# A hybrid state-space and attention layer on one core: taps made from tiles on the chip, bias loaded in halves, spreads by transpose, token tiles loaded in pairs

## The chip, the core and the metric

The kernel runs on one core of a Trainium2 chip. A core has five engines with queues of their own: TensorE (PE, matrix products; its weight loads are shown as PEld), VectorE (DVE), ScalarE (ACT), GpSimd (POOL) and SyncE (SP, which here only issues transfers). Each engine works through its own queue in order and waits on semaphores for the others. The metric is the device time of one execution in microseconds; lower is better. The profile shows one execution; its times count from the first instruction.

## The reference

One layer on 2048 tokens of 1024 features, in float32. `rmsnorm(x)` goes through one input projection, whose columns feed two groups:

```
h    = rmsnorm(x, g_mix);  proj = h @ w_in              # 2048 x 2048: u | q | k | v, 512 each
# group A: diagonal complex state space, 32 groups of 16 channels, 64 states each
lam_bar = exp(lam*dt);  b_bar = ((lam_bar-1)/lam) * B
states  = scan(lam_bar, u @ b_bar);  y = Re(states . C) + d*u
y    = gelu(y);  y = y * sigmoid(y @ w_glu + b_glu)
# group B: each frame attends to its 64-frame chunk and the 8 before it
s    = q.k/8 + rel_bias[head, clip(distance, -128, 128)]   # masked outside the band
att  = softmax(s) @ v                                       # 8 heads of 64
x    = x + concat(rmsnorm(y, g_ssm), rmsnorm(att, g_att)) @ w_out
h2   = rmsnorm(x, g_ffn)
x    = x + (silu(h2 @ w_gate) * (h2 @ w_up)) @ w_down        # inner width 2816
out  = rmsnorm(x, g_final)
```

## The kernel before

Tokens lie on the free axis in blocks of 512 (`SB`), features on the 128 partitions. A float32 operand is split into a high part (ACT, a cast) and a low part (VectorE, the difference), and a product is three matmuls (`mm3`, hi.hi, hi.lo, lo.hi). Small products and transposes are done on plain float32. Line 78 is the helper through which all products go, line 81 the one for transposes. PE's instructions keep the order in which the code emits them; the other queues are ordered by a planner, which may put anything forward whose inputs and buffers are free by its own estimate, except for the few instructions that are pinned.

Three stages matter here.

The **start** (`u_phase`) projects the state-space columns, blocks 1, 2, 3, 0. A block has four groups of 24 matmuls (`group`, banks `ps` or `pf`). Its token tiles `xt` (L440, `in_xp`) and its rows `x` for the sums of squares (L449) come from DRAM. When a block's root mean squares are known (`newton`), `spread` brings them from one column per 128 tokens onto all partitions: four products of the column, broadcast, with the identity, into a bank `pp`. Between the groups, `long(n)` advances `ssm_prologue`, which computes the state-space constants on VectorE: powers of the eigenvalues, the output side `v` (L337 to L345), the input side `wt` (L347 to L351), and, after the start, the powers `a8` on POOL (L353 to L364), the taps `kt` (the first eight values of the impulse response, products of `v` and `bb`, both reloaded from DRAM across partitions, L370 to L392) and the transposes of `wt` (L288 to L297), which are written to DRAM as `bst`. Also in the start, the negated bias (`nb`, 768 values per head) is spread out in DRAM to `nbm`, a 128 x 640 tile per head (L521), and two corners of each tile are set to 1e30 (L524).

The **attention** (`att_phase`) takes 128 steps (block, head pair, head of the pair, quarter block), in each of which PE does the scores `sc`, the transposes `pt` of an earlier step's probabilities and, at the end of a head, the product with the values (`pj`). `load_nb` (L798) loads the next head's bias tile two steps ahead. After a head pair, `pv_scale` (L875) spreads the reciprocals of the softmax sums with four products against the identity. Between these, units advance on a timetable: `hT_unit` loads, scales and splits the next block's token tiles (L695 to L707; two buffers `xt`, the first three tiles and the other five in two units), `qk_unit` and `v_unit` project, and eight `ssm_unit`s load (`U`, `Bst`, `Tm`, `Vm`, L549), multiply, scan on POOL (L587 to L599), move the result (`XG`, L621) and multiply again. The raw weights go through two buffers `raw` while block 0 is processed; later blocks reload the split weights `wss`. The pools of the attention take the memory that the prologue's pool gives back, and a tile there waits for the last use of what lay in its place; the values' tiles `v0` come first in it.

The **rest** (`mix_phase`, feed-forward and down projection) is touched only where it spreads root mean squares: `norm`, `rstd_steps`.

## Time and profile before

| | |
|---|---|
| time, median of 3 runs | 2327.94 us (2321.54 to 2329.34) |
| profiled execution | 2328.99 us, span 2327.2 us, mean granted clock 0.973 |
| PE busy | 2197.0 us of the span |
| VectorE, ACT, POOL busy | 1545.0, 1004.7, 349.0 us |
| start, to the last spread of the projection | 0 to 116.6 us |
| first scores to last scores of the attention | 142.7 to 756 us |
| moved by DMA | 434.90 MB |

A timeline row of the profile gives the start in us, the time in us, engine, line, operation, output and inputs by the program's names, shapes and a count; in brackets stands how long the engine had idled before and what it waited for. A row of waits gives who waited for what, the total in us, how often, and the longest. A row of DMA issues gives the queue, the count, the size of one and the median time from issue to landing. A row of a tile gives the shortest, median and longest duration in ns, and the first and last start. A row of windows gives the stretch, its length, each engine's busy time, the granted clock of PE as a share of full speed, the DMA engines' busy share and GB/s.

### The profile page before, as it was taken

The page shows a single profiled execution, that of the slowest core. Times are in us where ns is not written, and L with a number is a line of the kernel's source. Part 1 is how long each engine was busy: PE and PEld are TensorE (multiplying, and loading weights), DVE is VectorE, ACT ScalarE, POOL GpSimd, SP SyncE. Part 2 cuts the span into 40 slices and gives each one's busy share as a digit, 9 for nine tenths or more (in the row PEclk, how much of TensorE's full clock was granted, in tenths as well). Part 3 has the DMA queues.
Part 4 walks back from the last instruction along what each step waited for, and adds up shares of the span by engine and source line. Part 5 has one row for each costly group of instructions (what it writes and reads, how often), then busy time and mean ns, then how long its engine had stood idle before and what let it go on. Part 6 is the DMA issues. An engine that isn't in the chain of part 4 may idle for free.

```text
span 2327.2 us, 30433 instructions
## 1 busy us (share of the span) xinstructions
PE 2197.0 (94%) x10712; PEld 1852.3 (80%) x10712; DVE 1545.0 (66%) x2695; ACT 1004.7 (43%) x1655; POOL 349.0 (15%) x814
## 2 busy tenths in 40 slices
PE   8878899999997899999999999999999989999997
PEld 6766688898986688878888887888888878888886
DVE  7746545756545756777776668666756477789766
ACT  4435445555556752253333336333333343353321
POOL 3237545466542000000000000000000000000000
PEclk9989899999998999999999999999999999999998
DMA  8967676775654434763554647555423297465641
GB/s 274 291 221 249 194 209 196 200 221 176 193 153 146 141 105 149 245 198 127 182 180 149 235 160 284 183 198 163 167 90 114 68 338 255 163 216 186 227 158 73
DMA packets 225329, 434.90 MB, mean 187 GB/s; under 512 B 43480, under 2 KB 70152, under 8 KB 218072
## 3 DMA queue, kind: packets, MB, share of 16 engines
q1 hardware_dynamic: 220312, 418.79, 55.0%
q0 software_dynamic: 4864, 14.17, 1.9%
q8 instruction: 84, 1.38, 0.2%
q14 instruction: 69, 0.57, 0.1%
HBM read 292.88 MB, written 132.15 MB: 183 GB/s over the span
## 4 chain that ended last, share of the span: by engine, by line
PE 82%; DMA 6%; DVE 6%; POOL 2%; ACT 2%; issue 1%; SPq 1%; DVEq 0%; ACTq 0%; POOLq 0%
PE X L78 20%; PE ps L78 19%; PE Y L78 10%; PE pf L78 10%; PE big L78 9%; PE W L78 5%; PE pj L78 5%; PE sc L78 2%; PE pt L81 2%; DMA xt<-in_xp 2%; DMA xt<-in_xt 1%; DVE lo L154 1%; SPq L549 1%; DMA nb<-nbms 1%; DMA hd<-wc 0%
## 5 line engine op out<-in xcount | busy, mean ns | idle before, releaser
L78 PE MATMUL X<-hi,c 128*128 128x512 f32 x1408 | 451.3, 391 | 8.5 <-DVE c L154 6.9
L78 PE MATMUL ps<-hd,hd 128*128 128x512 f32 (+1 forms) x1968 | 432.0, 382 | 6.1 <-ACT hd L154 3.7
L78 PEld LDWEIGHTS ps<-hd,hd 128*128 128x128 f32 x1968 | 359.3, 190 | 77.5 <-ACT hd L154 4.6
L78 PEld LDWEIGHTS X<-hi,c 128*128 128x128 f32 x1408 | 265.6, 189 | 65.2 <-DVE c L154 7.8
L78 PE MATMUL X<-lo,c 128*128 128x512 f32 x704 | 274.9, 390 | 0.0
L154 ACT CAST hd<-hd 128x1536 fp32r<-128x1536 f32 (+1 forms) x106 | 147.6, 1393 | 238.1 <-DMA hd<-hq 181.9
L78 PE MATMUL Y<-hi,c 128*128 128x512 f32 x704 | 224.1, 389 | 1.5 <-DVE u L1367 1.5
L154 DVE TENSOR_TENSOR hd<-hd 128x1536 fp32r<-128x1536 f32 (+1 forms) x106 | 174.1, 1645 | 28.8 <-ACT hd L154 28.1
L154 DVE TENSOR_TENSOR c<-S,c 128x512 fp32r<-128x512 f32 x176 | 120.9, 688 | 104.1 <-ACT c L154 104.1
L829 DVE CUSTOM_DVE_ANT_0 s<-sc,nb 128x640 f32<-128x640 f32 (+4 forms) x128 | 94.5, 738 | 110.9 <-PE sc L78 98.7
L1491 DVE TENSOR_TENSOR acc<-acc,ps 128x512 f32<-128x512 f32 x196 | 131.3, 684 | 53.0 <-PE ps L78 48.3
L1363 ACT COPY u<-X 128x512 f32<-128x512 f32 x132 | 77.6, 588 | 204.9 <-PE X L78 204.8
L78 PE MATMUL big<-m,woh 128*128 128x512 f32 x512 | 162.7, 400 | 0.0
L78 PE MATMUL pf<-hi,w 128*128 128x512 f32 x416 | 153.1, 420 | 8.9 <-ACT w L154 4.6
L154 ACT CAST c<-S 128x512 fp32r<-128x512 f32 x176 | 109.5, 622 | 118.3 <-PE Y L78 67.0
L78 PEld LDWEIGHTS Y<-hi,c 128*128 128x128 f32 x704 | 132.1, 188 | 29.3 <-DVE u L1367 1.9
L78 PEld LDWEIGHTS X<-lo,c 128*128 128x128 f32 x704 | 132.8, 189 | 27.7
L154 ACT CAST c<-raw 128x512 fp32r<-128x512 f32 x132 | 82.2, 623 | 149.4 <-PE Y L78 71.2
L78 PE MATMUL Y<-lo,c 128*128 128x512 f32 x352 | 137.0, 389 | 0.0
L832 ACT ACTIVATE s<-s,mn 128x640 f32<-128x640 f32 (+4 forms) x128 | 98.0, 765 | 77.2 <-DVE mn L829 76.5
L848 DVE TENSOR_TENSOR ptl<-pt,pth 128x640 fp32r<-128x640 f32 (+3 forms) x152 | 98.3, 647 | 45.8 <-ACT pth L847 44.1
L847 ACT CAST pth<-pt 128x640 fp32r<-128x640 f32 (+3 forms) x152 | 83.7, 551 | 94.8 <-PE pt L81 89.5
(441 smaller groups left out, 4229.3 us busy)
## 6 DMA issues: line engine op xcount, KB each, us to landing
w<-wss SPq DMA_DIRECT2D x36, 1024.0 KB, 6.7
hq<-g SPq DMA_DIRECT2D x140, 256.0 KB, 2.2
hd<-hq SPq DMA_DIRECT2D x42, 768.0 KB, 4.4
hd<-wc SPq DMA_DIRECT2D x42, 768.0 KB, 6.0
raw<-in_w_gate SPq DMA_DIRECT2D x44, 512.0 KB, 3.7
raw<-in_w_up SPq DMA_DIRECT2D x44, 512.0 KB, 4.1
wc<-px SPq DMA_DIRECT2D x66, 256.0 KB, 3.2
wss<-w SPq DMA_DIRECT2D x12, 1024.0 KB, 6.0
```

What stands on the lines that cost most here:

```text
L78: return self.tc.keep_in_program_order(self.tc.nc.tensor.matmul(*a, **b))
L81: return self.tc.keep_in_program_order(self.tc.nc.tensor.transpose(*a, **b))
L154: return nc.scalar.copy(hi, raw), nc.vector.tensor_tensor(lo, raw, f32(hi), op=ALU.subtract)
L549: ins = nc.sync.dma_start(out, in_)
L829: nc.vector.tensor_tensor_reduce(s[:, :nk].rearrange("p (a b) -> p a b", a=nch), ps[:, :nch, :half], hd.nb[:, nk - 1 :: -1].rearrange("p ( ...
L832: nc.scalar.activation(s[:, :nk], s[:, :nk], AF.Exp, bias=mn[:], scale=-1.0, accum_out=sums[sb, pr][:, hh, qp : qp + 1])
L847: nc.scalar.copy(pth[:, a:b, qp, :], pt[:, a:b, :])
L848: nc.vector.tensor_tensor(ptl[:, a:b, qp, :], pt[:, a:b, :], f32(pth[:, a:b, qp, :]), op=ALU.subtract)
L1363: nc.scalar.copy(u[:], ps[:])
L1491: V.tensor_tensor(a, a, ps[:], op=ALU.add)
```

## The change

1. **Spreads.** `spread`, `rstd_steps` and `pv_scale` use a transpose of the broadcast column in place of the product with the identity.
2. **Taps.** They are made from the tiles in which VectorE computes `bbr`, `bbi` and `v`: for each group the real and the imaginary part are two products over 64 partitions that add up in one bank. The reloads of `bb` and `v` and the DRAM tensor `bb` go. The taps are now emitted between the projection groups, one block of eight groups behind the block of `v` that they read, and the transposes move up between the first q and k products. The transposed blocks 0 and 1 take the buffers of `v`, blocks 2 and 3 those of `bc` and `small`.
3. **Bias.** The DRAM tensor `nbm` goes. Two tiles on the chip hold a head's bias in turn; their corners are set once on POOL, and a head's values come straight from `nb` in two loads, one for each half of the partitions, whose rows overlap in DRAM. Head 0 is loaded in the start.
4. **Token tiles.** Of tiles 3 to 7 of a next block, 3 is loaded alone, 4 and 5 and then 6 and 7 as pairs into the buffers `raw`.

```diff
-LONG = 1, 3, 2
+VO, WI, TA = range(3)
+LONGS = ((VO, 0),), ((VO, 1),), ((TA, 0), (VO, 2)), ((TA, 1), (VO, 3)), ((TA, 2), (WI, 0)), ((TA, 3), (WI, 1)), ((WI, 2),), ((WI, 3),)
...
 def spread(k, te, pb, o, c):
     for i in range(4):
-        te.matmul(pb[:, i * P : (i + 1) * P], o[:, c + i : c + i + 1].to_broadcast([P, P]), k.ident[:], start=True, stop=True)
+        te.transpose(pb[:, i * P : (i + 1) * P], o[:, c + i : c + i + 1].to_broadcast([P, P]), k.ident[:])
...
-            bst = k.t(p, "v" if b_ > 1 else "vg", [P, 9 if b_ > 1 else 8, 2, NS], bufs=2)[:, :8]
+            bst = (k.t(p, "v", [P, 9, 2, NS], bufs=2) if b_ < 2 else k.t(p, ("bc", "small")[b_ - 2], [P, 8, 2, NS]))[:, :8]
...
+        def taps(b_):
+            kt = k.t(p, "kt", [CH, 8, P], bufs=2)
+            gs = slice(8 * b_, 8 * b_ + 8)
+            pss = [k.t(k.pro_psum, "pp", [P, 512])[:].rearrange("p (a b) -> p a b", a=4) for _ in range(2)]
+            for q in range(4):
+                for c, bt in enumerate((bbr, bbi)):
+                    for g2, ps in enumerate(pss):
+                        rows = slice(g2 * NS, (g2 + 1) * NS)
+                        k.te.matmul(ps[:CH, q, :], bt[rows, 4 * b_ + q, :], vts[b_][c][rows, q, :L, :].rearrange("p k c -> p (k c)"), start=c == 0, stop=c == 1)
+            for g2, ps in enumerate(pss):
+                nc.scalar.copy(kt[:, g2::2, :], ps[:CH])
+            V.tensor_tensor(kt[:, :, :CH], kt[:, :, :CH], dm[:, gs], op=ALU.add)
+            nc.gpsimd.dma_start(S["kt"][:, gs, 1], kt[:])
...
             if n == 1:
-                corner = k.t(p1, "corner", [64, 64])
-                nc.gpsimd.memset(corner[:], 1e30)
-                nc.sync.dma_start(S["nbm"][:], bass.AP(S["nb"].tensor, S["nb"].offset + 1, [[768, H], [1, P], [1, 640]]))
+                bias_corners(k, S["nba"])
+                bias_rows(k, S, 0, S["nba"])
...
-            long(LONG[n - 1])
+            long(1)
...
-            now += [group(b, f, f in pf) for f in (1, 2)]
+            for f in (1, 2):
+                now.append(group(b, f, f in pf))
+                if n > 1:
+                    long(1)
...
+def bias_rows(k, S, h, nb):
+    src = bass.AP(S["nb"].tensor, S["nb"].offset + h * 768 + 65, [[1, 64], [1, 576]])
+    k.nc.sync.dma_start(nb[:64, 64:], src)
+    k.nc.sync.dma_start(nb[64:, :576], src)
+    return nb
...
+            def load(q, n=1):
+                t = k.t(aw, "raw", [P, 1024], bufs=2) if n > 1 else k.t(aw, "xt", [P, SB], bufs=XB)
+                nc.sync.dma_start(t[:].rearrange("p (q t) -> p q t", q=n), io["xt"][q * P : (q + n) * P, ts].rearrange("(q p) t -> p q t", p=P))
+                for m in range(n):
+                    xts[q + m] = t[:, m * SB : (m + 1) * SB]
+            if q0 == 0:
+                load(0)
+                load(1)
+            else:
+                load(q0)
+                for q in range(q0 + 1, q1, 2):
+                    load(q, 2)
...
-                k.ta.matmul(pb[:, i * P : (i + 1) * P], rb[:, i].rearrange("p h d -> p (h d)"), ident[:], start=True, stop=True)
+                k.ta.transpose(pb[:, i * P : (i + 1) * P], rb[:, i].rearrange("p h d -> p (h d)"), ident[:])
```

More of the change, by code (lines that the diff above doesn't have):

```diff
@@ L140, in rstd_steps @@
     for i in range(nt):
-        te.matmul(pb[:, i * P : (i + 1) * P], o[:, i : i + 1].to_broadcast([P, P]), k.ident[:], start=True, stop=True)
+        te.transpose(pb[:, i * P : (i + 1) * P], o[:, i : i + 1].to_broadcast([P, P]), k.ident[:])
     k.nc.scalar.copy(out, pb[:, : nt * P])
@@ L330, in cc, with outputs @@
             return a[:, qs].unsqueeze(2).to_broadcast([P, 4, n, CH])
-        for g2 in range(2):
-            for c, bt in ((0, bbr), (1, bbi)):
-                nc.gpsimd.dma_start(S["bb"][:, g2, c].rearrange("q n m -> n q m"), bt[g2 * NS : (g2 + 1) * NS])
+        dm = k.t(p, "dm", [CH, NG, CH])
+        V.tensor_tensor(dm[:], ident[:CH, :CH].unsqueeze(1).to_broadcast([CH, NG, CH]),
+                        ddt[:].unsqueeze(2).to_broadcast([CH, NG, CH]), op=ALU.mult)
         yield
-        wts = []
+        kt = k.t(p, "kt", [CH, 8, P], bufs=2)
+        nc.gpsimd.memset(kt[:], 0.0)
         for b_ in range(4):
+            nc.gpsimd.dma_start(S["kt"][:, 8 * b_ : 8 * b_ + 8, 0], kt[:])
+        vts, wts = [], []
+        def taps(b_):
+            kt = k.t(p, "kt", [CH, 8, P], bufs=2)
+            gs = slice(8 * b_, 8 * b_ + 8)
[9 more added lines that the diff above has]
+            nc.gpsimd.dma_start(S["kt"][:, gs, 1], kt[:])
+        def outputs(b_):
             qs = slice(4 * b_, 4 * b_ + 4)
@@ L345, in ssm_prologue, with inputs @@
                                       vt[c][g2 * NS : (g2 + 1) * NS].rearrange("n q k c -> n q (k c)"))
-            yield
-        for b_ in range(4):
+            vts.append(vt)
+        def inputs(b_):
             qs = slice(4 * b_, 4 * b_ + 4)
@@ L351, in ssm_prologue @@
             wts.append(wt)
+        for make in LONGS:
+            for m, b_ in make:
+                (outputs, inputs, taps)[m](b_)
             yield
@@ L364, in ssm_prologue @@
             G.tensor_copy(S["sw"][:, n, 1, :], a8[:, 1, :, e])
-        kt = k.t(p, "kt", [CH, 8, P], bufs=2)
-        nc.gpsimd.memset(kt[:], 0.0)
-        for b_ in range(4):
-            nc.gpsimd.dma_start(S["kt"][:, 8 * b_ : 8 * b_ + 8, 0], kt[:])
-        bb = k.t(p, "bbg", [P, NG, CH])
-        nc.sync.dma_start(bb[:], S["bb"].rearrange("q g c n m -> (c n) (q g) m"))
-        dm = k.t(p, "cm1", [P, 576])[:CH, : NG * CH].rearrange("c (g m) -> c g m", g=NG)
-        V.tensor_tensor(dm, ident[:CH, :CH].unsqueeze(1).to_broadcast([CH, NG, CH]),
-                        ddt[:].unsqueeze(2).to_broadcast([CH, NG, CH]), op=ALU.mult)
-        vgs = []
-        for b_ in range(4):
-            vgs.append(k.t(p, "vg", [P, 8, P], bufs=2)[:] if b_ < 2 else k.t(p, "v", [P, 9, P], bufs=2)[:, :8])
-            nc.sync.dma_start(vgs[b_], S["v"].rearrange("q g c n m -> (c n) (q g) m")[:, 8 * b_ : 8 * b_ + 8, :P])
-        for b_ in range(4):
-            gs = slice(8 * b_, 8 * b_ + 8)
-            vg = vgs[b_]
-            kt = k.t(p, "kt", [CH, 8, P], bufs=2) if b_ < 2 else k.t(p, ("bc", "small")[b_ - 2], [CH, 8, P])
-            if b_ == 0:
-                yield
-            for g0 in (0, 4):
-                ps = k.t(k.pro_psum, "pp", [P, 512])[:].rearrange("p (a b) -> p a b", a=4)
-                for g in range(4):
-                    k.te.matmul(ps[:CH, g, :], bb[:, 8 * b_ + g0 + g, :], vg[:, g0 + g, :], start=True, stop=True)
-                nc.scalar.copy(kt[:, g0 : g0 + 4, :], ps[:CH])
-                yield
-            V.tensor_tensor(kt[:, :, :CH], kt[:, :, :CH], dm[:, gs], op=ALU.add)
-            nc.gpsimd.dma_start(S["kt"][:, gs, 1], kt[:])
+        yield
         for b_ in range(4):
@@ L518, in u_phase @@
             if n == 1:
-                corner = k.t(p1, "corner", [64, 64])
-                nc.gpsimd.memset(corner[:], 1e30)
-                nc.sync.dma_start(S["nbm"][:], bass.AP(S["nb"].tensor, S["nb"].offset + 1, [[768, H], [1, P], [1, 640]]))
-            if n == 3:
-                for m in range(2):
-                    corners = nc.sync.dma_start(S["nbm"][:, m * 64 : m * 64 + 64, m * 576 : m * 576 + 64].rearrange("h p c -> p h c"), corner[:].unsqueeze(1).to_broadcast([64, H, 64]))
-                    tc.keep_in_program_order(corners)
+                bias_corners(k, S["nba"])
+                bias_rows(k, S, 0, S["nba"])
             pf = FBANKS[n]
@@ L532, in u_phase @@
                 next(att)
-                long(1)
-            now += [group(b, f, f in pf) for f in (1, 2)]
+            for f in (1, 2):
+                now.append(group(b, f, f in pf))
+                if n > 1:
+                    long(1)
             sums(b)
@@ L537, in u_phase, with bias_corners @@
         finish(b, held)
-        long(7 - sum(LONG))
+        long(1)
     return pro, att
+def bias_corners(k, nb):
+    for m in range(2):
+        k.nc.gpsimd.memset(nb[m * 64 : m * 64 + 64, m * 576 : m * 576 + 64], 1e30)
+def bias_rows(k, S, h, nb):
[3 more added lines that the diff above has]
+    return nb
 def ssm_unit(k, p, psum, S, b, eng):
@@ L690, in hT_unit @@
             xts = {}
-            def load(q):
-                if q < q1:
-                    xts[q] = k.t(aw, "xt", [P, SB], bufs=XB)
-                    nc.sync.dma_start(xts[q][:], io["xt"][q * P : (q + 1) * P, ts])
-            for q in range(q0, q0 + 2):
-                load(q)
+            def load(q, n=1):
[10 more added lines that the diff above has]
+                    load(q, 2)
             for q in range(q0, q1):
                 yield
-                load(q + 2)
+                if q0 == 0 and q + 2 < q1:
+                    load(q + 2)
                 xt = xts[q]
@@ L704, in hT_unit @@
                     v.append(k.t(aw, f"{n}{q}x" if q < DB and sb % 2 else f"{n}{q}", [P, SB], F32R)[:])
-                nc.vector.scalar_tensor_tensor(xt[:], xt[:], k.gm[:, q : q + 1], S["rsn"][:, ts], op0=ALU.mult, op1=ALU.mult)
-                nc.scalar.copy(hi[q], xt[:])
-                nc.vector.tensor_tensor(lo[q], xt[:], f32(hi[q]), op=ALU.subtract)
+                nc.vector.scalar_tensor_tensor(xt, xt, k.gm[:, q : q + 1], S["rsn"][:, ts], op0=ALU.mult, op1=ALU.mult)
+                nc.scalar.copy(hi[q], xt)
+                nc.vector.tensor_tensor(lo[q], xt, f32(hi[q]), op=ALU.subtract)
             yield
@@ L794, in att_phase @@
             pass
-        nbs = {}
+        nbs = {0: S["nba"]}
         def load_nb(h):
-            nb = k.t(aa, "nb", [P, 640], bufs=2)
-            nc.sync.dma_start(nb[:], S["nbm"][h])
-            return nb
+            return bias_rows(k, S, h, nbt[h % 2])
         def scores(st):
@@ L900, in att_phase @@
         aa = cx.enter_context(tc.tile_pool(name="aa", reuse_waits="tile", bufs=1))
+        nbt = S["nba"], k.t(aa, "nbb", [P, 640])
+        bias_corners(k, nbt[1])
         sp = tc.alloc_tile_pool(name="ssm", reuse_waits="tile", bufs=1)
@@ L1586, in block_kernel @@
             "ya": k.t(dram, "ya_s", [NSB, DS, SB]), "x1": k.t(dram, "x1", [D, SEQ]),
-            "k": k.t(dram, "ks", [2, H, P, SB]), "nbm": k.t(dram, "nbms", [H, P, 640]), "nb": k.t(dram, "nbs", [H, 768]),
+            "k": k.t(dram, "ks", [2, H, P, SB]), "nb": k.t(dram, "nbs", [H, 768]),
             "bst": k.t(dram, "bsts", [4, P, 8 * P]), "v": k.t(dram, "vs", [NPR, 2, 2, NS, 9 * CH]),
@@ L1590, in block_kernel @@
             "hq": k.t(dram, "hq", [2, F2, 7, P, 512]), "wc": k.t(dram, "wc", [F2, 7, P, 512]), "wt": k.t(dram, "wt", [4, P, HALF]),
-            "bb": k.t(dram, "bbs", [NPR, 2, 2, NS, CH]), "kt": k.t(dram, "kts", [CH, NG, 2, P]),
+            "kt": k.t(dram, "kts", [CH, NG, 2, P]),
         }
@@ L1611, in block_kernel @@
             S["sw"] = k.t(p, "sw", [P, 3, 2, NPR])
+            S["nba"] = k.t(p, "nba", [P, 640])
             with tc.tile_pool(name="apf", bufs=2, space=bass.MemoryType.PSUM, reuse_waits="tile") as k.pfs:
```

## The prediction

> **What bounds the kernel now.** I read the busy line of the page first, then the list of what TensorE (PE) waited for up to 420 us, then the timeline at its longest waits: every edit but some transposes acts before 760 us.

> ```profile
> PE 2197.0 (94%) x10712; PEld 1852.3 (80%) x10712; DVE 1545.0 (66%) x2695; ACT 1004.7 (43%) x1655; POOL 349.0 (15%) x814
> PE sc L78 <- DVE mn L829: 14.8, 2, 13.6
> PE ps L78 <- ACT raw L442: 11.8, 2, 7.3
> ```

> PE is the bound, and idle for 130 of 2327 us. So an edit gains in two ways: fewer instructions on PE where PE is full, or a shorter wait in the start. Both waits listed are touched by the change, the second in part; the timeline shows where:

> ```profile
> 36.48 0.80 SPq L521 DMA_DIRECT2D nbms<-nbs  x1
> 63.17 1.38 ACT L442 ACTIVATE raw<-xt,g_mix 128x512 fp32r<-128x512 f32 x2 [14.55 <-DMA xt<-in_xp]
> 63.94 1.58 PE L78 MATMUL ps<-raw,wuh 128*128 128x512 f32 x2 [4.46 <-ACT raw L442]
> 75.84 1.06 PE L78 MATMUL pp<-ident,no 128*128 128x128 f32 x8
> 98.53 1.05 PE L78 MATMUL pp<-ident,no 128*128 128x128 f32 x8
> 99.34 0.48 PE L78 MATMUL ps<-hi,wuh 128*128 128x512 f32 x1
> 115.78 1.05 PE L78 MATMUL pp<-ident,no 128*128 128x128 f32 x8
> 143.24 0.33 PE L78 MATMUL sc<-hi2x,lo0x 128*128 128x128 f32 x1 [0.24 <-DMA lo0x<-lo0x]
> 160.13 0.55 PE L78 MATMUL sc<-hi2x,hi0x 128*128 128x256 f32 x1 [13.65 <-DVE mn L829]
> 165.91 0.48 PE L78 MATMUL pf<-w,hi 128*128 128x256 f32 x2
> 160.00:165.00 5.00, 4.87 (x23) 4.90 (x24) 0.43 (x2) 1.10 (x4) 0.00 (x0) 0.50 0.50 118
> ```

> The reader is to see three things. First, the bias is spread out in DRAM by one large transfer at 36.48; the token tiles queued behind it reach ACT so late that it idles 14.55 us. PE loses 4.46 us and then takes 11.9 us (63.94 to 75.84) for one group of products, where three fed groups take 16.4 (99.34 to 115.78), 5.5 each. Second, the first bias tile holds the second score product back by 13.65 us. Third, the granted clock (the third number from the end of the last row) is 0.50 after that gap though PE is busy, so the 5.8 us from 160.13 to 165.91 are nearly half lost too.

> **The change part by part.** *Roots and reciprocals by transposes.* A spread is four fp32 products, which the trace shows as eight instructions: 98.53 to 99.34, 0.81 us. The kernel's other transposes are single instructions:

> ```profile
> 497.38 0.71 PE L81 MATMUL pt<-ident,s 128*128 128x128 f32 x5
> 497.84 0.48 PE L78 MATMUL pf<-hi,w 128*128 128x512 f32 x1
> L78 PE MATMUL pj<-ident,rb x128: 270/275/377, 207.8 to 769.1; 128*128 128x128 f32 x128
> L78 PE MATMUL big<-ident,no x80: 271/275/553, 794.5 to 987.9; 128*128 128x128 f32 x80
> ```

> Five in 0.46 us, so four in 0.37, and a spread saves 0.44. By the code there are 16 of the reciprocals (128/8), 10 under big (80/8), 4 under pp, and 6 more: 36. Four belong to the start and are counted there; the four reciprocals of the first 300 us lie beside the scan on POOL (below) and count nothing. 28 x 0.44 = 12.3 us; bounds 8 (two thirds of it, if PE waits more elsewhere) and 36 x 0.44 = 16. [...]

> *Bias halves, the first part.* The transfer at 36.48 goes, and with it 4.46 + (11.9 - 5.5) = 10.9 us at most; two small loads and two memsets on POOL take its place. I take it all, as ACT only waited for the tiles; the other end is 0, if the tiles were late without it. The corners and the reloads of bb and v, on SP around 90 us, go as well; their worth is nothing, as PE has no wait there (99.34 to 115.78 is full), and SP's later loads can only come earlier.

> *Taps.* Before, a block of eight groups is eight products over 128 rows; after, sixteen over 64 rows, with the same 128 columns.

> ```profile
> 120.88 1.92 PE L78 MATMUL pp<-vg,bbg 128*16 128x128 f32 x16
> 122.73 0.50 PE L78 MATMUL pf<-hi,w 128*128 128x512 f32 x1
> 124.07 0.56 POOL L355 COPY a<-pr 128x16 f32<-128x16 f32 x1
> 141.63 1.18 POOL L392 DMA_DIRECT2D kts<-kt  x2
> 148.19 0.47 ACT L784 ACTIVATE v<-pf,no 128x256 fp32r<-128x256 f32 x1 [3.67 <-DMA kts<-bc]
> ```

> 16 instructions take 1.85 us, so a block's 32 take 3.7 and four blocks 14.8 (7.4 if pairs of 64 rows ran side by side; no row shows it, and I take the row's pace). They move from behind the last projection to between the projection groups, where PE is full. About 1 us more goes where block 2 follows a spread and needs the bank that ACT's copy still reads. Their inputs come from VectorE, each issued at least two projection groups ahead of PE (11 us); that is the cover, and without it PE would stand behind them in its fixed order. The copies of the taps and their sums move with them, off the path. Call T the start of the attention's first product, right behind the spread at 115.78: 115.78 + 0.81, 116.6 now. Then 116.6 - 10.9 - 3 x 0.44 + 14.8 + 1 = 120.2.

> *What is late next.* After T the taps' 7.4 us are gone, which alone brings the first scores (143.24, T + 26.6) to T + 19.2. But look at the last row. The values' tile lies on memory of the prologue, and its first copy waits for the last transfer out of the bc tile. That was the small kts one. After, blocks 2 and 3 of the transposed weights lie in bc and small, and their transfers stand on POOL's queue behind the powers, which run from 124.07 to 141.63 (T + 7.5 to T + 25). At 0.59 an issue bc goes out at T + 26.5. It lands between 5.3 us (kts<-bc) and 13.8 us (the slowest bsts, last number of the third row) later:

> ```profile
> kts<-bc POOLq DMA_DIRECT2D x1, 64.0 KB, 5.3
> bsts<-vg POOLq DMA_DIRECT2D x2, 512.0 KB, 8.5
> DMA to landing us min/median/max: 3.1/9.4/13.8
> ```

> I take 8.5, the row of the same size: T + 35, 155.2, and 0.5 for the copy. PE has two banks there, so it gets through the scores and value tiles 0 and 1 and then stands before value tile 2, which starts at 165.91 now. With 2.5 us for a cold start this point is in effect at 158: 8 us earlier. So of 10.9 + 13.65 + 2.5 us of removed waits, the taps and the new wait take back most. Bounds: 3 us (landing 13.8) to 17 us (no such wait: scores 3.8 us earlier, and 13 of the 13.65).

> *After that, POOL.* The scan of the first two state-space units takes as long as PE's work beside it, and *token tiles in pairs* act inside the second:

> ```profile
> 230.72 0.67 PE L78 MATMUL pj<-XG,Vm 128*128 128x256 f32 x2 [1.75 <-DMA XG<-X]
> 273.35 0.49 PE L78 MATMUL pf<-hi,w 128*128 128x512 f32 x1 [1.99 <-ACT hi L706]
> 279.26 0.79 PE L78 MATMUL pf<-hi,w 128*128 128x512 f32 x1 [2.29 <-ACT hi L706]
> 296.60 1.24 POOL L621 DMA_DIRECT2D XG<-X  x2 [0.30 <-POOL X L599]
> 304.35 0.59 PE L78 MATMUL pj<-XG,Vm 128*128 128x256 f32 x2
> XG<-X POOLq DMA_DIRECT2D x32, 127.5 KB, 4.3
> 420.77 0.41 PE L78 MATMUL sc<-k,q2h 128*128 128x320 f32 x1 [2.14 <-DVE k L753]
> 437.24 0.77 PE L81 MATMUL pt<-ident,s 128*128 128x128 f32 x5 [1.96 <-DVE ptl L848]
> 566.88 0.42 PE L78 MATMUL sc<-k,q2h 128*128 128x320 f32 x1 [2.38 <-DVE k L753]
> ```

> Tiles 4 to 7 no longer queue for two buffers: two pairs go into two others that stand idle by then. At 273 and 279 PE waits 4.3 us for them; but the scan's result (296.60 + 1.24 + 4.3 of landing) comes at 302.1 and is used at 304.35, so only 2.2 can come out. Of the three later waits, where VectorE's queue stands behind a late tile, I take 5.9 of 6.5. Together 8.1; from 2 to 11.

> *Bias halves, the second part.* 32 loads in the attention become 62, and 24 token loads 18: 24 more issues on SP.

> ```profile
> L800 SPq DMA_DIRECT2D nb<-nbms x32: 319/436/1827, 146.2 to 712.0; - x32
> nb<-nbms SPq DMA_DIRECT2D x32, 320.0 KB, 4.6
> L829 DVE CUSTOM_DVE_ANT_0 s<-sc,nb x128: 275/824/826, 159.7 to 756.1; 128x640 f32<-128x640 f32 x96, 128x128 f32<-128x128 f32 x8, 128x256 f32<-128x256 f32 x8, 128x384 f32<-128x384 f32 x8
> 326.34 1.97 PE L78 MATMUL pj<-U,Bst 128*128 128x256 f32 x8 [2.43 <-DMA Tm<-kts]
> ```

> 24 x 0.44 = 10.5 us of SP's time over 570 us. Behind them on SP stand the state-space loads, which PE does wait for, as in the last row; I charge 2 us (0 to 6). A bias load is issued two steps of 4.7 us (596/127) before its use and lands in 4.6: hidden.

> **Sum**, against the profiled execution (2328.99 us, span 2327.2, 1.05 above the median of the runs): 12.3 + 8 + 8.1 - 2 = 26.4, so 2302.6, and 2301.5 beside the median.

> **The rivals.** (a) *Taps side by side.* Alternate products use rows 0 to 63 and 64 to 127; if they overlap, T is 7.4 us earlier: 2294. For it: neighbours never share rows. Against it: each keeps its 128 columns and a weight load of its own. [...]

> (b) *Start and tiles give nothing.* The bst transfers land at their slowest or wait further, and POOL's scan and SP's order absorb the rest: 8 and 6.1 are lost, 2315.6. For it: POOL is already the last to arrive at 230.72.

> (c) *The spreads still cost two passes*, a broadcast column not being transposed in one, so that the change doesn't do what it says: 31 x 0.44 = 13.6 lost, 2315. Against it: the moving operand is the identity in both kinds of row.

> (d) *The halves come late* (slower). Each head's load becomes two transfers from overlapping DRAM rows. It decides when a head waits over 26.4/31 = 0.85 us, that is, when the halves land some 10.3 us after issue instead of 4.6; at 2 us a head the time is 2301.5 + 62 = 2363. For it: the first two loads held VectorE until 159.7. Against it: the bytes are fewer. [...]

> **How the numbers follow.** The forecast has 0.50 (own range 2296 to 2308), (a) 0.18, (b) 0.14, (c) 0.05, (d) 0.13. The range 2284 to 2322 leaves out (d) and thin tails: its low end is (a) with the start's upper bound, its high end (b) with SP's 6 us. A measurement here tells 0.3% (7 us, 2321 to 2335) from no change. The forecast, (a), (c) and 0.10 of (b) are faster, 0.83; 0.04 of (b) is the same; (d) is slower, 0.13.

> **What would show it.** The spreads appear as four transposes, 0.37 us from start to next. The wait for ACT raw near 60 us is gone. The taps stand between the projection groups, 3.7 us a block (1.9 under (a)), and T is near 120. The 13.65 us of sc are gone; in their place the copy into v waits for bsts<-bc or bsts<-small, and PE for that copy, until about 155. The waits for hi near 273 and 279 shrink, and XG is waited for near 295. The prediction is wrong if POOL's queue has bsts ahead of the powers (then 2293), or if nb appears among VectorE's waits at many heads.

## The result, and the profile after

The changed kernel takes 2297.82 us (median of 4 runs, 2291.46 to 2300.86) against 2327.17 us for the kernel before on the same chip: a ratio of 0.9874, 95% interval 0.9847 to 0.9901, so 29.3 us less. A second set of five runs, with runs of the kernel before beside it, gave 2293.45 us against 2330.61, ratio 0.9836 (0.9813 to 0.9859), 37.2 us less. The forecast was 2301.5, or 26.4 less. The profiled execution of the changed kernel, 2291.46 us, is the fastest of its four, so the pair of profiles shows more (span 2327.2 to 2289.7, 37.5) than the medians do.

First the busy line of the page and three waits from the list of what TensorE (PE) waited for (total, times, longest, in us); then PE's, POOL's, ScalarE's (ACT) and SP's timelines where the prediction had its steps.

```profile
PE 2176.4 (95%) x10632; PEld 1833.7 (80%) x10632; DVE 1544.3 (67%) x2695; ACT 1000.6 (44%) x1655; POOL 350.4 (15%) x813
PE pt L82 <- DVE ptl L867: 12.0, 7, 3.3
PE sc L79 <- DVE hi2x L774: 4.1, 1, 4.1
PE sc L79 <- DMA lo0x<-lo0x: 2.9, 1, 2.9
```

```profile
62.27 0.60 PE L82 MATMUL pp<-ident,no 128*128 128x128 f32 x4
62.63 0.71 PE L79 MATMUL ps<-raw,wuh 128*128 128x512 f32 x2
69.69 0.28 PE L79 MATMUL pp<-v,bbr 64*16 64x128 f32 x1 [1.00 <-ACT pb L479]
78.13 0.87 PE L79 MATMUL pp<-v,bbr 64*16 64x128 f32 x4 [0.84 <-ACT kt L355]
100.82 0.40 PE L79 MATMUL pp<-v,bbr 64*16 64x128 f32 x4
102.67 0.50 PE L79 MATMUL ps<-hi,wuh 128*128 128x512 f32 x1
114.06 0.48 PE L79 MATMUL pf<-hi,w 128*128 128x512 f32 x1
132.90 0.45 PE L79 MATMUL sc<-hi2x,hi0x 128*128 128x128 f32 x1 [4.07 <-DVE hi2x L774]
133.56 0.63 POOL L298 DMA_DIRECT2D bsts<-bc  x1
136.25 0.47 PE L79 MATMUL sc<-hi2x,lo0x 128*128 128x128 f32 x1 [2.91 <-DMA lo0x<-lo0x]
136.94 0.59 POOL L298 DMA_DIRECT2D bsts<-small  x1
142.04 0.47 ACT L805 ACTIVATE v<-pf,no 128x256 fp32r<-128x256 f32 x1 [4.40 <-PE pf L79]
145.42 0.48 PE L79 MATMUL pf<-w,hi 128*128 128x256 f32 x2
187.78 0.60 PE L82 MATMUL pj<-ident,rb 128*128 128x128 f32 x4
188.22 0.38 PE L82 MATMUL pt<-ident,s 128*128 128x128 f32 x2
252.97 0.50 PE L79 MATMUL pf<-hi,w 128*128 128x512 f32 x1 [3.16 <-ACT hi L727]
282.03 0.67 PE L79 MATMUL pj<-XG,Vm 128*128 128x256 f32 x2 [1.61 <-DMA XG<-X]
394.50 0.48 PE L79 MATMUL sc<-k,q2h 128*128 128x320 f32 x1 [2.08 <-DVE k L774]
411.41 1.03 PE L82 MATMUL pt<-ident,s 128*128 128x128 f32 x5 [2.84 <-DVE ptl L867]
540.16 0.42 PE L79 MATMUL sc<-k,q2h 128*128 128x320 f32 x1 [3.11 <-DVE k L774]
```

The reader is to see five things. A spread is four transposes, 0.36 us in the start (62.27 to 62.63) and 0.44 in the attention (187.78 to 188.22). The last block of taps takes 1.85 us for its 32 instructions (16 products, two instructions each; 100.82 to 102.67), not 3.7; the first two blocks stand still for ScalarE (1.00 and 0.84). The 13.65 us at the second score product are gone, and the copy into the values' tile (142.04) waits for PE, not for the transposed weights, which left between POOL's powers at 133.56 and 136.94. PE now waits 4.07 and 2.91 us for the first q and k. And the three later waits that the token pairs were to shorten are all still there, at 394.50, 411.41 and 540.16.

Where the profiled pair parts, as start times in us of the same instruction in both timelines:

| start of | before | after | difference | difference in the second profile of the changed kernel |
|---|---|---|---|---|
| second spread of the start | 75.8 | 62.3 | -13.6 | -13.3 |
| attention's first product (T) | 116.6 | 114.1 | -2.5 | -0.9 |
| value tile 2 | 165.9 | 145.4 | -20.5 | -19.9 |
| second state-space unit, first product | 248.5 | 227.8 | -20.7 | -17.9 |
| third state-space unit, first product | 326.3 | 300.8 | -25.5 | -22.9 |
| output stage's first spread | 794.5 | 765.1 | -29.4 | -25.8 |
| first product of the feed-forward | 1011.4 | 975.3 | -36.0 | -33.0 |

So some 20 us come before value tile 2, some 5 between the second and third state-space units, 3 in the rest of the attention and 7 in the output stage.

### The profile page after: what moved, and what is told of

Read it like the earlier page. It is cut to its first block, busy times and chain, and to the rows that moved or that the text cites. A ratio compares the mean times of both kernels' runs of the same rounds, so it can differ in the third digit from the quotient of the medians.

```text
span 2289.7 us, 30275 instructions
## 1 busy us (share of the span) xinstructions
PE 2176.4 (95%) x10632; PEld 1833.7 (80%) x10632; DVE 1544.3 (67%) x2695; ACT 1000.6 (44%) x1655; POOL 350.4 (15%) x813
## 4 chain that ended last, share of the span: by engine, by line
PE 83%; DVE 4%; DMA 3%; issue 2%; ACT 2%; POOL 2%; SPq 1%; DVEq 0%; POOLq 0%; ACTq 0%
PE X L79 20%; PE ps L79 20%; PE Y L79 10%; PE pf L79 9%; PE big L79 9%; PE W L79 5%; PE pj L79 4%; PE sc L79 2%; PE pt L82 2%; SPq L563 1%; SPq L648 0%; POOL X L604 0%; DVE ptl L867 0%; ACT ys L1027 0%; DMA lo<-hc 0%
## 5 line engine op out<-in xcount | busy, mean ns | idle before, releaser
L79 PEld LDWEIGHTS Y<-hi,c 128*128 128x128 f32 x704 | 132.2, 188 | 29.7 <-DVE u L1388 2.2
L79 PE MATMUL W<-hi,c 128*128 128x512 f32 x352 | 115.5, 389 | 0.0
## 6 DMA issues: line engine op xcount, KB each, us to landing
raw<-in_w_gate SPq DMA_DIRECT2D x44, 512.0 KB, 3.7
raw<-in_w_up SPq DMA_DIRECT2D x44, 512.0 KB, 4.3
```

What stands on the lines that cost most here:

```text
L79: return self.tc.keep_in_program_order(self.tc.nc.tensor.matmul(*a, **b))
```

## The experiments

Ratios are to the kernel before on the same chip. The first four kernels ran together; for the others, which had no neighbour of their own, the changed kernel's ratio is taken as 0.9836 to 0.9874, the two measured. All times in the table are starts in us, from one profile each.

| kernel | second spread | T | value tile 2 | second unit | third unit | feed-forward | median, ratio (interval) |
|---|---|---|---|---|---|---|---|
| changed, again | 62.5 | 115.7 | 146.0 | 230.6 | 303.4 | 978.3 | 2293.45, 0.9836 (0.9813-0.9859) |
| spread_products | 62.7 | 116.1 | 146.7 | 230.8 | 302.0 | 994.8 | 2311.99, 0.9915 (0.9898-0.9932) |
| taps_same_rows | 63.7 | 117.1 | 148.6 | 231.0 | 303.1 | 982.9 | 2297.27, 0.9855 (0.9836-0.9874) |
| tiles_single | 61.9 | 113.2 | 144.2 | 225.8 | 305.3 | 983.7 | 2301.36, 0.9869 (0.9851-0.9887) |
| spread_transfer | 71.0 | 119.5 | 149.8 | 234.1 | 306.9 | 982.2 | 2298.12, 0.9862 (0.9845-0.9880) |
| bst_behind_powers | 64.2 | 114.6 | 147.9 | 232.5 | 305.8 | 982.5 | 2298.12, 0.9856 (0.9829-0.9883) |
| bias_one_half | 63.3 | 111.8 | 142.3 | 224.5 | 297.4 | 971.3 | 2288.93, 0.9820 (0.9799-0.9841) |
| transposes_behind | 63.0 | 114.2 | 148.7 | 230.6 | 303.1 | 977.4 | 2297.77, 0.9861 (0.9842-0.9880) |
| taps_old | 63.7 | 107.0 | 141.2 | 228.1 | 302.9 | 980.2 | 2298.11, 0.9867 (0.9848-0.9886) |
| bias_old | 73.0 | 122.4 | 153.6 | 233.3 | 305.5 | 984.6 | 2297.95, 0.9863 (0.9845-0.9881) |
| bb_stores | 63.0 | 114.0 | 145.0 | 226.7 | 299.1 | 980.2 | 2295.48, 0.9854 (0.9834-0.9874) |
| bias_second_queue | 62.6 | 113.2 | 143.9 | 231.3 | 308.3 | 995.7 | 2318.20, 0.9952 (0.9934-0.9970) |

A single profile of one kernel differs from another by up to 3 us from value tile 2 on (the changed kernel's two do), so a difference of that size in one cell says nothing.

**The changed kernel again.**

> The changed kernel itself, so that the others have a neighbour on the same chip. Its earlier runs gave 2291.5 to 2300.9 us, the profiled one 2291.5. If the 8 us that the profiled run gained between the first spread of the output stage (765) and the first product of the feed-forward (978), where the ten spreads account for 4.4, are of the change, this run shows them again: 212 to 213 us from one to the other. If they are chance, it shows 216 to 217 and a time near 2298.

From the output stage's first spread (768.7) to the feed-forward it took 209.7 us, and 210.2 in the first profile (765.1 to 975.3), against 216.9 before (794.5 to 1011.4). The gain of 7 is of the change: ten spreads are 4.5 of it; a wait for a squared sum shrinks from 0.60 to 0.25, and one of 1.41 at the first feed-forward product is gone. In the kernel with the spreads as products, below, these two places have waits of 0.60 and 1.59 again. The 212 to 213 in the expectation ended at a later product: to that one it took 212.5 here, 212.9 in the first profile and 221.0 before.

**The spreads as products.**

```diff
-        te.transpose(pb[:, i * P : (i + 1) * P], o[:, c + i : c + i + 1].to_broadcast([P, P]), k.ident[:])
+        te.matmul(pb[:, i * P : (i + 1) * P], o[:, c + i : c + i + 1].to_broadcast([P, P]), k.ident[:], start=True, stop=True)
```

(and in `rstd_steps` and `pv_scale` alike)

> All 36 spreads are products with the identity again, all else is as in the changed kernel. The prediction's step: 12.3 us slower than the changed kernel (28 spreads of 0.44), 6 to 7 of it in the attention. Rival: the attention is paced there by VectorE and ScalarE as much as by TensorE, so the 16 spreads behind the head pairs return little; then it is 5 to 8 us slower, nearly all of it in the output stage.

It is 18.5 us slower than its neighbour, on the forecast's side and beyond it. One spread of a head pair, in its timeline and then in that of the kernel before, with the instruction behind it:

```profile
188.78 1.05 PE L79 MATMUL pj<-ident,rb 128*128 128x128 f32 x8
189.67 0.38 PE L82 MATMUL pt<-ident,s 128*128 128x128 f32 x2
```

```profile
207.78 1.05 PE L78 MATMUL pj<-ident,rb 128*128 128x128 f32 x8
208.67 0.38 PE L81 MATMUL pt<-ident,s 128*128 128x128 f32 x2
```

0.89 us against 0.44 after: 0.45 saved each, 16.2 for 36. By the two intervals the difference is 12 to 25 us. By stretches: from T to the third state-space unit this kernel takes 185.9 us and the changed one 186.7 and 187.7, so the first spreads return nothing, as forecast; from there to the output stage 475.4 against 464.3 and 465.3; in the output stage 217.4 against 210.2 and 209.7. The rival, 5 to 8 in all and nearly all of it in the output stage, falls on the time. The 11 us of the middle stretch are not all spreads, as the kernel before, with the same spreads, takes 468.2 there, and this profile is of the slowest of the kernel's five runs (2320.27); so what the spreads return in the attention is not settled. The 7.5 of the output stage come with the spreads, as the kernel before takes 216.9.

**Taps with neighbours on the same rows.**

```diff
-            for q in range(4):
-                for c, bt in enumerate((bbr, bbi)):
-                    for g2, ps in enumerate(pss):
+            for g2, ps in enumerate(pss):
+                for q in range(4):
+                    for c, bt in enumerate((bbr, bbi)):
```

> The 32 products of a block of taps in another order: first the 16 over rows 0 to 63, then the 16 over rows 64 to 127. If neighbours on different rows ran side by side, a block takes 3.5 us in place of 1.75 and the kernel is 7 us slower, with the attention's first product 7 us later. Rival: a product over 64 rows costs half of one over 128 whatever stands beside it; then a block still takes 1.75 us and nothing changes (within 2 us).

The same 32 instructions, the last block, in this kernel's timeline:

```profile
102.57 0.39 PE L79 MATMUL pp<-v,bbr 64*16 64x128 f32 x2
105.74 0.50 PE L79 MATMUL ps<-hi,wuh 128*128 128x512 f32 x1
```

3.17 us, against 1.85 with the rows alternating. So here products on different halves of the rows ran side by side, and the rival with half the cost for half the rows falls; in the changed kernel's timeline two instructions start at 69.69, the next two at 69.81. (The neighbours on different rows also write different banks; no run separates the two.) The alternating order is 1.7-fold faster (3.17 to 1.85). But the kernel's T is only 1.4 to 3 us later and its time 3.8 us longer, less than the intervals tell apart. From the second spread to T it takes 53.4 us, the changed kernel 51.8 and 53.2: in this order the blocks don't meet the wait for the second bank (1.00 above, 2.70 in the second profile), and most of the 5.3 us (4 x 1.32) falls into waits that are there anyway.

**Token tiles one by one.**

```diff
-                for q in range(q0 + 1, q1, 2):
-                    load(q, 2)
...
+            for q in range(q0, q0 + 2):
+                load(q)
             for q in range(q0, q1):
                 yield
-                if q0 == 0 and q + 2 < q1:
-                    load(q + 2)
+                load(q + 2)
```

> Token tiles 3 to 7 of a next block one by one through two buffers, as in the kernel before. The prediction's step: 8.1 us slower than the changed kernel, with VectorE's waits for these tiles back at 16 us and TensorE's waits near 273 and 279 (now 253) back. Rival: these waits of VectorE lay where TensorE had other work, and the later waits for k come from the splitting itself, which stands ahead of it on VectorE; then 0 to 4 us slower.

It is 7.9 us slower than its neighbour, as the step said, but not where the step said. Its PE waits in block 1, and those of the changed kernel there:

```profile
250.87 0.49 PE L79 MATMUL pf<-hi,w 128*128 128x512 f32 x1 [3.12 <-ACT hi L720]
255.84 0.80 PE L79 MATMUL pf<-hi,w 128*128 128x512 f32 x1 [2.65 <-ACT hi L720]
265.70 0.49 PE L79 MATMUL pf<-hi,w 128*128 128x512 f32 x1 [2.28 <-ACT hi L720]
```

```profile
252.97 0.50 PE L79 MATMUL pf<-hi,w 128*128 128x512 f32 x1 [3.16 <-ACT hi L727]
255.01 0.80 PE L79 MATMUL pf<-hi,w 128*128 128x512 f32 x1 [0.58 <-ACT hi L727]
```

From the second to the third state-space unit it takes 79.6 us (225.75 to 305.33) where the changed kernel takes 73.0 and 72.8: 6.5 to 6.8 us, in block 1. The kernel before takes 77.9 there, so not all of this is what the pairs saved against it. From there to the feed-forward it takes 678.4, the changed kernel 674.5 and 674.9, but these 3.7 us are spread out: of the three later waits one is gone here and the others are 2.15 and 2.73 long, against 2.08 and 3.11. On this the rival was right: those waits come from the splitting itself, which stands ahead of k on VectorE, with single tiles and with pairs (in the changed kernel VectorE is busy with it from 537.24 to 539.39, then makes k, and PE's product starts at 540.16). (By the two intervals the 7.9 us are 1 to 15.)

**The bias transfer back in the start, unused.**

```diff
             if n == 1:
+                nc.sync.dma_start(S["nbm"][:], bass.AP(S["nb"].tensor, S["nb"].offset + 1, [[768, H], [1, P], [1, 640]]))
                 bias_corners(k, S["nba"])
```

> The changed kernel with the large transfer of the bias from DRAM to DRAM put back at its old place in the start; nothing reads what it writes. The prediction's step: it was this transfer that made the token tiles late, so ScalarE waits over 10 us for a tile again, the second spread of the start moves from 62.3 to about 75, the attention's first product from 114 or 116 to about 126, and the kernel is 10 to 12 us slower. Rival: the token tiles came earlier for another reason (the order of the loads, the reloads that went); then under 3 us.

The mechanism is there, its worth is not. ScalarE's wait for the token tiles, in this kernel:

```profile
59.73 0.72 ACT L445 ACTIVATE raw<-xt,g_mix 128x512 fp32r<-128x512 f32 x1 [15.39 <-DMA xt<-in_xp]
```

The slowest load of these tiles took 15.1 us to land (8.2 in the changed kernel, 25.5 before), and the second spread came at 71.0, 8.6 us late. But T is only 4 to 5 us late, and the time is within the changed kernel's two ratios. Between the second and the third spread the changed kernel takes 29.7 us, this one 26.5 (97.4 - 71.0): a PE that comes early stands before the taps, most of it for ScalarE's copies (2.6 and 3.1 us of waits in the two profiles of the changed kernel, 0.4 here), so about half of the gain ahead of them was not PE's to keep.

**The transposed weights behind the powers.**

```diff
-            nc.gpsimd.dma_start(S["bst"][b_], ...)
+            k.tc.keep_in_program_order(nc.gpsimd.dma_start(S["bst"][b_], ...))
...
-            G.tensor_copy(S["sw"][:, n, 1, :], a8[:, 1, :, e])
+            k.tc.keep_in_program_order(G.tensor_copy(S["sw"][:, n, 1, :], a8[:, 1, :, e]))
```

> The four transfers of the transposed weights are held behind the last power on POOL's queue, where the prediction had put them; in the changed kernel they stand between the powers. The prediction's step: the last two leave at about 141 to 143, land 8 us later, the first copy into the values' tile waits for them until about 150, and TensorE stands before value tile 2 until then, 5 us later than now (145.4): 5 us slower, or what the later stages leave of it. Rival: the copy doesn't wait for these transfers; then nothing changes (within 2 us).

A wait appears, smaller, and not at the place forecast. Value tile 2 starts 33.4 us after T (147.95 - 114.59), against 31.4 and 30.3: 2 to 3 us, not 5. The copy waits only 0.34 us for bsts<-bc, which landed in 6.3 us, not 8.5, and PE does not stand for that copy: it waits 1.91 us for VectorE's first scores, which start at 143.99 (136.77 in the changed kernel). At 143.97 a memset on POOL starts that has waited 4.09 us for bsts<-v, an earlier block's transfer; VectorE's tile seems to wait for the same, though the profile doesn't name it. The median shows nothing beyond the uncertainty.

```profile
138.83 0.53 POOL L298 DMA_DIRECT2D bsts<-bc  x1
145.21 0.47 ACT L805 ACTIVATE v<-pf,no 128x256 fp32r<-128x256 f32 x1 [0.34 <-DMA bsts<-bc]
```

**One half of the bias only.**

```diff
-            return bias_rows(k, S, h, nbt[h % 2])
+            if nbt_n[h % 2] == 0:
+                nbt_n[h % 2] = 1
+                return bias_rows(k, S, h, nbt[h % 2])
+            nb = nbt[h % 2]
+            nc.sync.dma_start(nb[:64, 64:], bass.AP(S["nb"].tensor, S["nb"].offset + h * 768 + 65, [[1, 64], [1, 576]]))
+            return nb
```

> Left out: from the third head on, a head's bias is loaded into the upper half of the partitions only, and the lower half keeps the values of an earlier head. 30 issues on SP go. The prediction's step: 24 issues cost 2 us (0 to 6), so this is 2.5 us faster than the changed kernel. Rival: the issues lie beside other work; then no difference (within 2 us). If it were over 6 us faster, halves that come late (the prediction's slower rival) would be at work in part.

From T to the feed-forward it takes 859.5 us, the changed kernel 861.3 and 862.7: 1.8 to 3.2 for 30 issues. That fits the forecast's 2.5, but two profiles of one kernel differ by up to 3 us in a single start. By the ratios it is 4 to 13 us faster, and the 4 are within the uncertainty; a part is a T of 111.8, 2 to 4 us early, which this edit doesn't explain. It isn't settled whether the rest is chance.

**The transposes behind the first q and k.**

```diff
-PRO = 0, 0, 2, 2, 2, 2, 0, 0, 0
+PRO = 0, 0, 0, 0, 0, 0, 0, 0, 0
```

> The 32 transposes of the weights stand behind the first q and k products, as before the change, in place of between them. TensorE then has them to do while the first q and k are copied, where it now waits 4.1 and 2.9 us. Theory: they were the cover of that wait, so the first scores come 3 us earlier (from 18.8 to about 15.7 after the attention's first product), and the kernel is up to 3 us faster. Rival: the transfers out of bc and small then leave about 8 us later and the first copy into the values' tile waits for them, which takes the 3 us back or makes it up to 3 us slower.

The rival, in part. The waits for q and k shrink (2.01 and 0.94, before the transposes and the first scores), but the first scores come only 0.5 us earlier after T, and then the copy, VectorE's first scores and PE wait:

```profile
143.54 0.47 ACT L805 ACTIVATE v<-pf,no 128x256 fp32r<-128x256 f32 x1 [9.70 <-DMA bsts<-bc]
142.27 0.29 DVE L848 CUSTOM_DVE_ANT_0 s<-sc,nba 128x128 f32<-128x128 f32 x1 [7.17 <-DMA bsts<-v]
142.62 0.58 PE L79 MATMUL sc<-hi2x,hi0x 128*128 128x256 f32 x1 [6.71 <-DVE mn L848]
```

Value tile 2 is at T + 34.5. The copy's wait is the one that the prediction had put into the changed kernel, with the place and the releaser that it named (the transfers out of bc and small leave 4.9 and 2.0 us later than in the changed kernel, where the rival had 8). PE's is not: it stands behind VectorE (mn), whose score tile waits for the transfer out of v, which the prediction had not counted.

**The taps of the kernel before.** The functions `transposes` to the end of `ssm_prologue` are those of the kernel before, with its schedule `LONG` and the reloads of bb and v; the rest is as after.

> Spreads, bias halves and token pairs as in the changed kernel, the taps as in the kernel before: bb and v go through DRAM, the products stand behind the last projection, the taps' last tiles lie in bc and small. Prediction's step: the moved taps cost 15.8 us ahead of the attention's first product and save 7.4 behind it, and their stored weights bring a wait of about 5 before value tile 2; so this kernel would be 8 to 13 us faster than the changed one. By the runs so far (pairs side by side, 12 us of taps with their waits, no wait at the values): 3 to 6 us faster. Rival: the stores and reloads of bb and v crowd the token tiles of the start, which takes that back: no difference, or slower by up to 5.

T is 7 to 9 us earlier and value tile 2 4 to 5 us, so up to there the moved taps cost what the second of the theories said. The lead is gone 90 us later, or 2.5 us of it are left: the second state-space unit starts at 228.1 (227.8 and 230.6 in the changed kernel), the third at 302.9 (300.8 and 303.4), and the time is that of the changed kernel. PE's waits in between:

```profile
209.81 1.19 PE L78 MATMUL pj<-XG,Vm 128*128 128x256 f32 x2 [3.85 <-DMA XG<-X]
228.08 2.40 PE L78 MATMUL pj<-U,Bst 128*128 128x256 f32 x8 [2.24 <-DMA Tm<-kts]
```

Before the products with POOL's scan result PE waits 3.85 us (1.25, put down to a bias load, in the changed kernel's first profile, 3.28 in its second), and before SP's loads for the next unit 2.24 (1.34 and 1.01). Behind the wait of 3.85 the granted clock is 0.50 from 210 to 215, where it is 1.00 in the first profile; behind that of 3.28 it is 0.53 from 215 to 220. These waits, and the clock behind them, take most of the lead back. The rival's cause is not supported: the second spread stands at 63.7, so the stores of bb don't crowd the start.

**The bias of the kernel before.**

```diff
-                bias_corners(k, S["nba"])
-                bias_rows(k, S, 0, S["nba"])
+                corner = k.t(p1, "corner", [64, 64])
+                nc.gpsimd.memset(corner[:], 1e30)
+                nc.sync.dma_start(S["nbm"][:], bass.AP(S["nb"].tensor, S["nb"].offset + 1, [[768, H], [1, P], [1, 640]]))
...
-            return bias_rows(k, S, h, nbt[h % 2])
+            nb = nbt[h % 2]
+            nc.sync.dma_start(nb[:], S["nbm"][h])
+            return nb
```

(the corners go to DRAM as before; the two tiles stay where the changed kernel has them)

> The bias as in the kernel before (spread out in DRAM in the start, corners there, one load per head), all else as in the changed kernel. Prediction's step: the transfer in the start and the wait of 13.65 us for the first bias tile return, less 2 us for the SP issues saved; with 4 us for the transfer, which the run with the unused transfer showed, this is 14 to 18 us slower than the changed kernel. Rival: the first bias tile is late only because SP reaches it late, and the wait for it shrinks with the shorter queue: 3 to 8 us slower.

Within the uncertainty of the changed kernel, so the step's 14 to 18 us are not there, and the rival's 3 to 8 are not told from nothing. The second spread is 10.6 us late (73.0), T 7 to 8, value tile 2 again 8; but there is no wait of 13.65 us. The first load of the bias, on SP, in this kernel and in the kernel before:

```profile
94.05 0.34 SPq L826 DMA_DIRECT2D nba<-nbms  x1
```

```profile
146.23 3.20 SPq L800 DMA_DIRECT2D nb<-nbms  x2
```

Both read the same DRAM tensor. Before, the tile lay on memory that the prologue's pool gives back; its load went out at 146.23, behind SP's other issues and with no wait of its own over 0.3 us, and landed 13.3 us later. Here the tile has memory of its own, the load goes 52 us earlier and lands in 2.9. So the way through DRAM does not bring the wait by itself. The place of the tile on the chip, which lets the planner put the load forward, is the likely cause; no run moved the tile alone, and why the load took 13.3 us to land is not shown. After value tile 2 the 8 us shrink, to 3 to 6 at the second unit (233.3).

**The stores of bb back, unused.**

```diff
+        for g2 in range(2):
+            for c, bt in ((0, bbr), (1, bbi)):
+                nc.gpsimd.dma_start(S["bb"][:, g2, c].rearrange("q n m -> n q m"), bt[g2 * NS : (g2 + 1) * NS])
```

> The four stores of bb to DRAM, in rows of 64 bytes, put back on POOL's queue at their old place, with nothing that reads them. In the kernel with the unused bias transfer the second spread of the start came at 71.0, in the kernel before at 75.8, in the changed one at 62 to 64: 8 of 13 us were the transfer's. Theory: these stores are most of the rest, so the second spread comes at 66 to 67 and the attention's first product 1 to 3 us later. Rival: they cost the start nothing (62 to 64), and the rest is the order of the loads on SP.

The second spread stands at 63.0: the theory falls. What made the second spread of the kernel before (75.8) later than in the two kernels with the bias transfer (71.0 and 73.0) stays open; the first spread is late there already (41.8, against 39.4 and 41.3), which can be 2.5 and 0.5 us of the 4.9 and 2.8.

**The second half of the bias from ScalarE's queue.**

```diff
-    k.nc.sync.dma_start(nb[64:, :576], src)
+    k.nc.scalar.dma_start(nb[64:, :576], src)
```

> The second half of each head's bias is loaded from ScalarE's queue in place of SP's, all else as in the changed kernel. SP has 32 issues fewer, as in the run that left the second half out, which from the attention's first product to the first of the feed-forward took 2 to 3 us less. Theory: SP's issues cost that, and it is kept here: 2 to 3 us faster. Rival: ScalarE's queue is in order, its 32 issues of about 0.45 us and their waits for VectorE hold back its casts, and it is as fast or slower by up to 10 us.

2318.2 us, 20 to 25 us slower than the changed kernel's medians, beyond even the rival. T and value tile 2 are as early as ever; it loses some 4 us by the second unit, and more at single places, one of which is this. SP's timeline here, and the same eight loads and stores in the changed kernel:

```profile
504.22 5.52 SPq L648 DMA_DIRECT2D y<-X  x8
509.85 7.98 SPq L563 DMA_DIRECT2D U<-u  x8
517.87 0.45 SPq L563 DMA_DIRECT2D Tm<-kts  x1
```

```profile
492.44 3.78 SPq L648 DMA_DIRECT2D y<-X  x8
496.32 3.83 SPq L563 DMA_DIRECT2D U<-u  x8
500.20 3.78 SPq L563 DMA_DIRECT2D Tm<-kts  x8
```

The eight issues of U take 7.98 us in place of 3.83 (also 8.02 for seven and 7.50 for eight in two other units; behind the first unit the changed kernel's longest are 5.53 and 5.36), and PE then waits 5.18 us for Tm. In the list of its waits, PE's for Tm grew from 8.2 to 14.7 us, and VectorE stood 9.1 us for one bias tile. Why SP's issues became slower is not shown.

## Why the prediction came out right, step by step

**Spreads** (12.3 us): right, and sized low. 0.45 us each, and those beside POOL's scan count nothing, both as forecast; but the ten of the output stage return 7 us and not 4.4, because two waits there shorten too. The run without them says 18.5 (12 to 25). In the start a spread went from 0.81 to 0.36 us, 2.25-fold.

**Start** (up to 10.9 us): the second spread gained 13.6; the transfer is 8.6 of it by the run that puts it back. The step failed on what follows: PE comes that much earlier and waits at the taps, 2.6 and 3.1 us in the two profiles, where the prediction had 1 us. The cover that it named, VectorE's inputs "two projection groups ahead (11 us)", held but for 0.33 us; the rest is ScalarE's copies out of the banks.

**Taps** (14.8 + 1): this term failed; rival (a) was right. Pairs run side by side, 1.85 us a block. With their waits the four blocks took 12.3 us: from the second spread to T the changed kernel takes 51.8, the kernel before 40.8, less 1.3 for three spreads (53.2 and 13.7 by the second profile). T was 114.1 and 115.7, forecast 120.2. That (a) holds made the kernel hardly faster, though, as its run in the other order shows.

**The new wait at the values' copy** (most of what reduced the start to 8 us net): it didn't come. The prediction had named POOL's queue with the transposed weights ahead of the powers as what would make it wrong, and that is what the planner did, between them. Held back, the weights do make value tile 2 late, by 2 to 3 us, but in the path the prediction was wrong even there: PE waits for VectorE's first scores, not for the copy. So value tile 2 gained 20 us and not 8.

**The 13.65 us**: gone, but not by the halves, as the run with the bias through DRAM lacks the wait too; the first tile's own memory is what is left, by argument and not by a run. The step took two edits for one.

**What is late next**: the first scores start at T + 18.8, forecast T + 19.2. The moved transposes had covered the copies of q and k: with them behind, PE's two waits are 2.01 and 0.94 us in place of 4.07 and 2.91. Behind those waits the granted clock was a half again, by the windows of the changed kernel (the third number from the end is PE's clock):

```profile
136.50:142.00 5.50, 5.50 (x27) 5.50 (x28) 0.30 (x2) 0.49 (x2) 2.47 (x9) 0.50 1.00 336
```

It fell already in the first of them, of 4.07 us: PE is idle from 128.83, and the granted clock is 1.00 from 130 to 131, 0.94 from 131 to 132 and 0.50 from 132 to 142. Half of the 5.5 us from 136.50 to 142.00, 2.75, is an estimate of what it cost.

**Token pairs** (8.1 us): 7.9 measured, from two errors that cancel. Against the run with single tiles, 6.5 to 6.8 us came out in block 1 where 2.2 were forecast. Against the kernel before the limit held: POOL's scan, taken as a fixed end at 302, moved forward with its unit. Its last result leaves 47.6 and 47.7 us after the unit's first product, 48.1 before; PE waits 1.61 us for it in one profile and uses it 54.3 and 53.4 us after that product, 55.9 before, so 1.6 and 2.5 came out ahead of it. The single tiles have 60.2 there, more than the kernel before; why is not shown. The 5.9 us of later waits stayed: VectorE's splitting ahead of k (2.15 us, from 537.24 to 539.39) is work, not a late tile.

**SP's issues** (-2 us): in line with 1.8 to 3.2 for 30, though two profiles of one kernel differ by up to 3 in a single start. **Rival (d)**, halves that come late: not in this kernel, as no wait of PE or VectorE for a bias tile over 1.3 us is listed; the run with two queues shows it can be had (9.1 us for one tile).

**The sum**, by stretches, forecast against the two profiles of the changed kernel (us saved against the profile of before):

| stretch | forecast | measured |
|---|---|---|
| to value tile 2 | 8 | 20.5, 19.9 |
| to the third state-space unit | 2.2 (tiles) | 5.0, 3.0 |
| to the output stage | 9.2 (5.9 tiles, 5.3 spreads, -2 SP) | 3.9, 2.9 |
| output stage | 4.4 | 6.6, 7.2 |
| the rest | 2.6 | 1.5, 2.5 |
| sum | 26.4 | 37.5, 35.5 |

The start was forecast 12 us too low, for the taps and for the wait that didn't come, the later part of the attention 6 too high, for the waits for k that stayed. So it is in part luck that the sum came near the first median. The medians, 29.3 and 37.2 less, say that a profile catches a good run as easily as a middling one. What the forecast lacked altogether is that a lead at value tile 2 is only partly kept: 4 to 5 us more with the taps of before, 8 less with the bias of before, and neither kernel's time differs from the changed one's beyond the uncertainty. Put back one at a time, only the spreads (18.5 us) and, barely, the token tiles (7.9) cost time; no run puts the wait of 13.65 us back, so what its end is worth in the whole time is not shown.

No run that computes everything is faster than the changed kernel beyond the uncertainty. What the runs point to, and was not tried, is memory of their own for the transposed weights, in v as well as in bc and small, with the transposes behind the first q and k.

## What to carry to other kernels

A gain ahead of a stage that another queue paces is worth what that stage leaves of it (with the taps of before, a lead of 4 to 5 us at value tile 2 was 2.5 or none at the second unit): ask at which point the two meet next (here the scan's result and the loads of the next unit) before counting it. When a wait names a transfer, look at when that transfer was allowed to start; and a tile laid on memory given back late can wait for the last reader of that memory (7.17 us, for bsts<-v, in the run with the transposes behind). An operation saved on a nearly full engine (PE, 95% busy) was worth its time where that engine didn't stand for another behind it, so count all of those places: the spreads beside POOL's scan returned nothing (185.9 us from T to the third unit with the products, 186.7 and 187.7 with the transposes), those of the output stage 7 us.

## What the runs showed of the hardware that was not expected

```profile
L82 PEld LDWEIGHTS pj<-ident,rb x64: 138/140/145, 187.6 to 738.9; 128*128 128x128 f32 x64
```

```profile
L78 PEld LDWEIGHTS pj<-ident,rb x128: 186/192/192, 207.6 to 769.0; 128*128 128x128 f32 x128
```
